# Buffers at multiples of 64 bytes, later triangular solves, two low parts on VectorE and modulation slabs first, in a hybrid transformer layer

## The chip, the cores and the metric

The kernel runs on one NeuronCore of a Trainium2 chip. The metric is the device time of one execution in microseconds (us), lower is better. The kernel before takes 1467.25 us, the median of 3 runs (1467.24 to 1467.57).

## The reference, cut to what matters

One layer mixes a latent stream of 1024 tokens and a context of 256 tokens, width 1024, all in fp32. `w_in` projects the normalised input to three head groups; `w_out` joins them; a squared-ReLU MLP of width 4096 follows.

```python
mod = silu(c) @ w_mod + b_mod            # six rows of 1024: sh1, sc1, g1, sh2, sc2, g2
h = rms(x, norm1) * (1 + sc1) + sh1      # the same for the context with c_ctx
P = project(h, w_in)                     # f (256) | aq (512) | ak, av (128 each) | dq, dk, dv (256 each) | dz (256) | gates (16)
# Gated DeltaNet on dq, dk, dv: centred conv + SiLU, chunks, one scan per direction
tmat = triangular_solve(eye + lmat, eye) # lmat from k k^T and the decays
o_dn = scan over the chunks, in both directions, from the context's final state
o_att = softmax(q k^T / 8) v             # 8 query heads, 2 kv heads, over latent and context keys
x = x + g1 * (concat(dft2(f), o_att, gated_norm(o_dn)) @ w_out)
x = x + g2 * (relu(h2 @ w_ff1) ** 2 @ w_ff2)
```

## The kernel before, in words

**Number format.** A product in near-fp32 is made of three matmuls in the fast format fp32r: each operand is split into a high part (the value rounded to fp32r) and a low part (what is left), and `mm3` (L238) issues high by high, high by low and low by high into one PSUM bank. In the trace they are L239, L240 and L241. A matmul streams its moving operand (the right one of `mm`/`mm3`, up to 512 columns) past 128 columns of weights (the left one).

**Memory.** Four regions of SBUF hold everything. `fbase` (FW words of 4 bytes) and `rbase` (RW words, fp32r) lie one behind the other, `z1a` (later `z1b`, `z1c`, `z1d`; Z1W words) follows them, `z2a` (later `z2b`, `z2c`; Z2W words) is laid against the upper end. Each is an `Arena`, which hands out buffers at multiples of 8 words, that is 32 bytes (`words`, L115). In the built program `fbase` begins at byte 16512 of a partition, so `rbase` begins at 16512 + 4 x 16200 = 81312, `z1a` at 81312 + 4 x 18704 = 156128, and `z2a` at 190432. Only `fbase` begins at a multiple of 64; the three others lie 32 bytes past one, and the operands of all fp32r matmuls are in these three. Their buffers there have sizes of whole multiples of 64 bytes, so each moving operand and each block of weights begins 32 bytes past a multiple of 64, either at 32 or at 96 of 128.

**Stages**, in the order of time (us of the profiled span):

- 0 to 60: the modulation. `w_mod` comes as slabs of 128 rows by 1024 columns (512 KB each), eight for each of the six output rows (`mod_steps`, L314); a slab feeds four matmuls of 256 columns (L321 is its DMA). The first two row blocks of x are loaded (`load_x`, L362, DMA L365), normalised (`norm_in`) and transposed (L244, into `xTb`) between the slabs of the first output row (q = 0), whose result is sh1; q = 1 gives sc1. From both comes `hT`, the modulated input, transposed, high and low.
- 60 to 200: the projections of `w_in`. `wgroup` (L434) loads a group of 256 or 272 columns in two halves, ScalarE makes the high part (`act`, L223), and the engine `eng` the low part (a subtraction of 128 x 1024, L446). `proj_N` (L474) and `proj_T` (L463) are the matmul loops; each calls `tick` (L453), which advances the generators in `tasks`.
- From the second half of the query columns on, `tasks` has `systems` (L764) and `system1` (L772). `systems` first yields GRAM = 4 times, then makes the Gram blocks of the keys (`grams`: matmuls L734 of 32 x 32, scaled on VectorE in L737, sent to DRAM), then solves the triangular systems of direction 0 on VectorE; `system1` waits for the Gram blocks and solves direction 1 on GpSimd. Each solve (`solve`, L745) has 30 steps of a product (L758) and a sum (L759), first for the context (32 partitions), then for the latent tokens (128 partitions). Beside them VectorE, GpSimd and ScalarE normalise and rotate the query rows (`qk_rows`, L502: L508 to L520).
- 200 to 340: `w_dv` and `w_dq`, the value and query columns of the DeltaNet group, with low parts on GpSimd (`wgroup(..., G)`), their convolutions (L594 to L603 on VectorE, matmuls L627), then the columns dz and f (`wfz`, `dz_f`), whose group f is prepared once both solves of the context and the 4 first steps of `dz_f` are issued.
- 340 to 705: attention (scores of 256 columns, values of 512 columns by 65 weights, row maxima of 512 columns, all fp32r in `rbase`) with the DeltaNet scan (fp32 matmuls of 32 to 64) in between.
- 705 to 850: `w_out` (moving operand in `z1c`, 256 columns) and the Fourier group. 850 to 1155: the first MLP product (weights in `z1c`, moving operand in `rbase` or `z2b`, 512 columns). 1155 to 1450: the second (both in `rbase`, 512 columns).

**What sets the order.** A scheduler orders the instructions of each engine by program order, priorities and its own estimate of when operands are ready; matmuls under `pinned` and DMAs under `ypin` keep the order of the program. Each engine then works off its queue in order, and an instruction that waits holds all behind it.

Of the kernel before, what the change touches and what calls it, by code (L numbers as in the profile page):

```python
# [17 lines left out]
P = 128  # L18
D = 1024
# [3 lines left out]
KT = D // P  # L23
# [7 lines left out]
NCC = CTX // CK  # L31
NCA = NCL + NCC
EPS = 1e-6
FW, RW, Z1W, Z2W = 16200, 18704, 8576, 9728

COL_F, COL_AQ, COL_AK, COL_DQ, COL_DK, COL_DV, COL_DZ, COL_G = 0, 256, 768, 1024, 1280, 1536, 1792, 2048

# [2 lines left out]
NGP = ((0, 3), (122, 140))  # L40
OFF = 800
OFN = 1000
GRAM = 4
PIN = lambda i: i
HOPS = (0, 5, 7, 9, 10, 11, *range(13, 33, 2))
FIRST = 2
# [63 lines left out]
class Arena:  # L110
# [2 lines left out]
        self.typed = base.dtype  # L113

    def words(self, n, top=False):  # L115
        n = (n + 7) // 8 * 8
        order = range(len(self.free_) - 1, -1, -1) if top else range(len(self.free_))
        for q in order:
            a, b = self.free_[q]
            if b - a >= n:  # L120
                if top:
                    at = b - n
                    self.free_[q] = (a, at)
                else:
                    at = a
                    self.free_[q] = (a + n, b)
                self.used[at] = n
                self.peak = max(self.peak, sum(self.used.values()))
                return at
        raise RuntimeError(f"arena full: {n} words, free {self.free_}, used {sorted(self.used.items())}")  # L130
# [64 lines left out]
def body(tc, t, out):  # L195
# [3 lines left out]
    with ctx:  # L199
# [9 lines left out]
        zp2, Z2 = zone("right", Z2W, F32, "z2a")  # L209
# [4 lines left out]
        V, G, T, Y, SC = nc.vector, nc.gpsimd, nc.tensor, nc.sync, nc.scalar  # L214

        def buf(*shape, top=False, a=None, at=None):
            return Buf(a or Fa, (P,) + shape, top, at)
# [14 lines left out]
        def yd(i):  # L232
            return tc.keep_in_program_order(i) if ypin else i

        def mm(o, l, r, start, stop):
            pe(T.matmul(o, l, r, start=start, stop=stop))  # L236
# [37 lines left out]
        cs = csb()  # L274
# [10 lines left out]
        at = 16  # L285
# [24 lines left out]
        def mod_pass(*a):  # L310
            for _ in mod_steps(*a):
                pass

        def mod_steps(q, slabs, bank, queue=Y, many=1):  # L314
            w = t["w_mod"]
            for k in range(KT):
                sl = slabs.next()
                sl = sl if isinstance(sl, tuple) else (sl,)
                n = D // len(sl)
                for z, part in enumerate(sl):  # L320
                    yd(queue.dma_start(part, w[0, k * P : (k + 1) * P, q * D + z * n : q * D + (z + 1) * n]))  # L321
                for g in range(4):
                    mm(bank[32 * g : 32 * g + 32, 0:256], cs[:, k, :], sl[g * 256 // n][:, g * 256 % n : g * 256 % n + 256], k == 0, k == KT - 1)
                if k % many == many - 1:
                    yield

# [12 lines left out]

        rowtmp = buf(256)  # L340
        slab0 = [buf(D, a=Z2) for _ in range(8)]
        slabs = Ring([b() for b in slab0])

# [60 lines left out]
        ypin = True  # L406
        xs0 = load_x(t["x"][0], 0, xb[0:2])
        norm_in(xs0)
        slab1 = [buf(D, a=Z2)]
        xTb = [buf(256) for _ in range(KT)]  # L410
        trb = Ring([bk[0], bk[1]])
        slabs = Ring([b() for b in slab0 + slab1])
        for k, _ in enumerate(mod_steps(0, slabs, bk[2])):
            b = trb.next()
            for q, xt in enumerate(xs0):
# [74 lines left out]
        ypin = False  # L490
# [60 lines left out]
        for p, xs in enumerate((xs1, xs2, xs3, xs4)):  # L551
            norm_in(xs)
            g, c0 = ((0, 256), (1, 0), (1, 256), (2, 0))[p]
# [108 lines left out]
        b = gb.next()  # L662
# [9 lines left out]
        b = gb.next()  # L672
# [8 lines left out]
        b = gb.next()  # L681
# [5 lines left out]
        for d in range(2):  # L687
# [3 lines left out]
            for c in range(0, NCA, 16):  # L691
                n = min(16, NCA - c)
# [103 lines left out]
            proj_N(w_q, 256, range(NT), q_sink(half))  # L796
        for b in [x for r in rt.items for x in r] + rst.items + stg.items + [gqk]:
            b.free()
        w_dv = wgroup([(COL_DV, 256)], G)
        conv_proj(w_dv, 0, (0, 1, 2))  # L800
        dst = conv_silu(0, 4, (0, 1, 2), "v", 0)
        conv_proj(w_dv, 1, (0, 1, 2))
# [5 lines left out]
        wlo.items.append(rbuf(4, 256, a=Z1))  # L808
        wb += [whi.items[-1], wlo.items[-1]]
        whi.at = wlo.at = 2  # L810
        w_dq = wgroup([(COL_DQ, 256)], G)
        conv_proj(w_dq, 1, (0, 1))
        compact(dst, 1, VC, 0.5)
        G.tensor_tensor(VC, VC, NK[:, 0].unsqueeze(2).to_broadcast([P, NCA, HD]), op=ALU.mult)
# [987 lines left out]
```

## Time and profile before

| | |
|---|---|
| median of 3 runs | 1467.25 us |
| the profiled execution | 1465.56 us |
| its span | 1463.8 us |
| mean granted TensorE clock | 0.979 |
| TensorE busy (matmuls) | 1385.7 us, 95% of the span |
| VectorE, ScalarE, GpSimd busy | 1003.7, 704.8, 673.4 us |
| bytes moved by DMA | 197.67 MB, 135 GB/s over the span |

The span is what the profiler saw from the first to the last instruction; the execution is 1.8 us longer than it. Busy time of a matmul row runs from its issue to its modelled end, and rows overlap: 0.39 us is one matmul's length, but what it takes of the engine is the distance between two starts. The columns of a table by stretch are busy us of PE, PEld, DVE, ACT and POOL (with instruction counts), the granted TensorE clock (1.00 is 2.4 GHz, 0.50 is 1.2 GHz), the DMA engines' busy share and GB/s.

### The profile page before, as it was taken

Reading aid. Unit: us, or ns where it says so; the run is one execution under the profiler, and the core shown is the slowest. Engines: PE = TensorE matmul, PEld = TensorE weight load, DVE = VectorE, ACT = ScalarE, POOL = GpSimd, SP = SyncE. Lnnn points to the kernel's source line nnn. Section 1 sums busy time; section 2 is a strip of 40 time slices with the busy share of each in tenths; the row PEclk is TensorE's granted clock in tenths of the full one; section 3 lists DMA queues with packets and bytes.
Section 4 is the critical chain, followed back from the end, with each engine's and each line's share of the span. In section 5 each row is a group of like instructions: output and inputs, shape, how many; then the busy total and the mean of one; then the engine's idle time right before and its main releaser. Section 6 shows DMA issues by size and latency. Waiting matters only on the chain.

```text
span 1463.8 us, 28936 instructions
## 1 busy us (share of the span) xinstructions
PE 1385.7 (95%) x11462; PEld 1119.9 (77%) x11462; DVE 1003.7 (69%) x1691; ACT 704.8 (48%) x1239; POOL 673.4 (46%) x743
## 2 busy tenths in 40 slices
PE   5899968899999999989899899999999999999998
PEld 1677967676777777768799777888888888888886
DVE  0774589965888777786723788655556677676994
ACT  1742412233777777767512664555455443443331
POOL 2653778783446456465533724444433100010782
PEclk8899989899999999999999999999999999999999
DMA  8873151233000010042222215544446897766641
GB/s 315 315 271 123 34 115 36 66 85 90 9 10 24 9 32 10 9 149 64 84 93 93 104 60 163 178 130 149 150 159 205 302 394 263 245 225 219 201 159 58
DMA packets 137304, 197.67 MB, mean 135 GB/s; under 512 B 45021, under 2 KB 80463, under 8 KB 136911
## 3 DMA queue, kind: packets, MB, share of 16 engines
q1 hardware_dynamic: 136464, 195.12, 40.8%
q8 instruction: 90, 1.47, 0.4%
q10 hardware_dynamic: 703, 0.69, 0.2%
q14 instruction: 47, 0.39, 0.1%
HBM read 149.84 MB, written 45.94 MB: 134 GB/s over the span
## 4 chain that ended last, share of the span: by engine, by line
PE 48%; DVE 2%; POOL 2%; DMA 1%; issue 1%; ACT 0%; DVEq 0%; SPq 0%; POOLq 0%; ACTq 0%
PE bk L240 8%; PE bk L239 8%; PE bk L241 8%; PE ba L239 7%; PE ba L240 7%; PE ba L241 7%; PE bk L236 2%; DVE z1b L1333 0%; PE ba L236 0%; POOL rbase L1468 0%; DMA fbase<-x 0%; PE bk L244 0%; DVE rbase L996 0%; POOL z2c L1734 0%; POOL z2c L1732 0%
## 5 line engine op out<-in xcount | busy, mean ns | idle before, releaser
L223 ACT ACTIVATE rbase<-fbase 128x512 fp32r<-128x512 f32 (+3 forms) x255 | 171.7, 686 | 88.0 <-PE bk L240 55.6
L223 ACT ACTIVATE fbase<-bk 128x512 f32<-128x512 f32 (+3 forms) x224 | 125.0, 561 | 142.7 <-PE bk L236 94.0
L236 PE MATMUL bk<-rbase 128*128 128x256 f32 (+2 forms) x984 | 173.1, 311 | 4.6 <-ACT fbase L223 2.5
L236 PEld LDWEIGHTS bk<-rbase 128*128 128x128 f32 (+1 forms) x984 | 132.2, 175 | 34.2 <-ACT fbase L223 3.3
L236 PE MATMUL ba<-rbase 128*65 128x512 f32 (+4 forms) x576 | 138.4, 342 | 6.2 <-DVE rbase L996 4.8
L223 ACT ACTIVATE z1c<-fbase 128x512 fp32r<-128x512 f32 (+1 forms) x120 | 76.7, 653 | 134.9 <-DMA fbase<-w_ff 51.0
L223 ACT ACTIVATE fbase<-fbase 128x512 f32<-128x512 f32 (+4 forms) x148 | 96.0, 659 | 91.9 <-POOL fbase L1624 27.5
L1501 POOL TENSOR_TENSOR fbase<-fbase 128x512 f32<-128x512 f32 x64 | 87.4, 1367 | 114.5 <-DVE z1c L1468 89.5
L1706 POOL TENSOR_TENSOR z2c<-z2c,fbase 128x512 f32<-128x512 f32 x16 | 31.1, 1968 | 204.6 <-ACT z2c L223 128.5
L972 DVE TENSOR_REDUCE fbase<-ba 128x1 f32<-128x512 f32 (+1 forms) x192 | 106.4, 593 | 19.5 <-PE ba L236 18.1
L223 ACT ACTIVATE rbase<-z1d 128x1024 fp32r<-128x1024 f32 x61 | 63.0, 1055 | 101.3 <-PE bk L240 86.6
L1468 DVE TENSOR_TENSOR z1c<-fbase,z1c 128x512 fp32r<-128x512 f32 x112 | 91.2, 818 | 24.0 <-ACT z1c L223 20.8
L1468 DVE TENSOR_TENSOR rbase<-z1d,rbase 128x1024 fp32r<-128x1024 f32 x61 | 85.1, 1411 | 27.7 <-ACT rbase L223 27.2
L996 POOL TENSOR_TENSOR rbase<-fbase,rbase 128x512 fp32r<-128x512 f32 x56 | 72.1, 1288 | 67.0 <-ACT rbase L223 62.9
L239 PE MATMUL bk<-rbase 128*128 128x512 f32 x256 | 99.6, 389 | 0.0
L240 PE MATMUL bk<-rbase 128*128 128x512 f32 x256 | 99.6, 389 | 0.0
L241 PE MATMUL bk<-rbase 128*128 128x512 f32 x256 | 99.6, 389 | 0.0
L996 DVE TENSOR_TENSOR rbase<-fbase,rbase 128x512 fp32r<-128x512 f32 x104 | 81.5, 784 | 25.5 <-ACT rbase L223 25.1
L1468 DVE TENSOR_TENSOR rbase<-fbase,rbase 128x1024 fp32r<-128x1024 f32 (+1 forms) x65 | 81.3, 1269 | 21.2 <-ACT rbase L223 21.0
L236 PEld LDWEIGHTS ba<-rbase 128*65 128x65 f32 (+1 forms) x576 | 76.1, 155 | 24.1 <-DVE rbase L996 5.9
L240 PE MATMUL ba<-rbase 128*128 128x512 f32 x192 | 74.7, 389 | 0.0
L241 PE MATMUL ba<-rbase 128*128 128x512 f32 x192 | 74.7, 389 | 0.0
(350 smaller groups left out, 3823.5 us busy)
## 6 DMA issues: line engine op xcount, KB each, us to landing
fbase<-w_ff SPq DMA_DIRECT2D x70, 512.0 KB
u<-fbase SPq DMA_DIRECT2D x112, 256.0 KB
z2a<-w_mod SPq DMA_DIRECT2D x36, 512.0 KB
z1d<-w_ff SPq DMA_DIRECT2D x34, 512.0 KB
z1d<-u SPq DMA_DIRECT2D x33, 512.0 KB
fbase<-u SPq DMA_DIRECT2D x23, 512.0 KB
fbase<-w_in SPq DMA_DIRECT2D x16, 512.0 KB
fbase<-x SPq DMA_DIRECT2D x14, 512.0 KB
```

The source lines that it names most:

```text
L223: return SC.activation(o, i, f, **k)
L236: pe(T.matmul(o, l, r, start=start, stop=stop))
L239: pe(T.matmul(o, lh, rh, start=start, stop=False))
L240: pe(T.matmul(o, lh, rl, start=False, stop=False))
L241: pe(T.matmul(o, ll, rh, start=False, stop=stop))
L972: V.tensor_reduce(st4[:, z : z + 1], b, AX.X, ALU.max)
L996: (G if k2 in GP and not any(a <= n < b for a, b in NGP) else V).tensor_tensor(hl[:, :, 1], p, f32(hl[:, :, 0]), op=ALU.subtract)
L1468: eng.tensor_tensor(lo, i, f32(hi), op=ALU.subtract)
L1501: G.tensor_tensor(w[nm], w[a], w[b], op=op)
L1706: G.tensor_tensor(c, c, G2[cs_.start // 512], op=ALU.mult)
```

## The change

Four edits.

1. **Addresses.** FW is 16192 and Z2W is 9736, and an arena hands out buffers of 64 words or more at multiples of 16 words (64 bytes). `rbase` now begins at 81280, `z1a` at 156096, `z2a` at 190400, all multiples of 64, so every operand of an fp32r matmul moves 32 bytes down, from 32 or 96 of 128 to 0 or 64 of 128. Which pairs of moving operand and weights have the same place of 128, and which differ by 64, stays as it was.
2. **Later solves.** GRAM is 15.
3. **Low parts.** `w_dv` and `w_dq` use the default engine of `wgroup`, VectorE: four subtractions (L446) leave GpSimd.
4. **Slabs first.** The ninth slab buffer is there from the start, and the eight slabs of q = 0 are loaded ahead of the first row blocks of x.

```diff
-FW, RW, Z1W, Z2W = 16200, 18704, 8576, 9728
+FW, RW, Z1W, Z2W = 16192, 18704, 8576, 9736
...
-GRAM = 4
+GRAM = 15
...
     def words(self, n, top=False):
+        unit = 16 if n >= 64 else 8
         n = (n + 7) // 8 * 8
         order = range(len(self.free_) - 1, -1, -1) if top else range(len(self.free_))
         for q in order:
             a, b = self.free_[q]
-            if b - a >= n:
-                if top:
-                    at = b - n
-                    self.free_[q] = (a, at)
-                else:
-                    at = a
-                    self.free_[q] = (a + n, b)
+            at = (b - n) // unit * unit if top else -(-a // unit) * unit
+            if at >= a and at + n <= b:
+                self.free_[q : q + 1] = [x for x in ((a, at), (at + n, b)) if x[0] < x[1]]
...
+        early = {}
+
+        def slab_load(q, k, slabs, queue=Y):
+            sl = slabs.next()
+            yd(queue.dma_start(sl, t["w_mod"][0, k * P : (k + 1) * P, q * D : (q + 1) * D]))
+            return sl
+
         def mod_steps(q, slabs, bank, queue=Y, many=1):
-            w = t["w_mod"]
             for k in range(KT):
...
+                sl = slab_load(q, k, slabs, queue) if (q, k) not in early else early.pop((q, k))
                 for g in range(4):
-                    mm(bank[32 * g : 32 * g + 32, 0:256], cs[:, k, :], sl[g * 256 // n][:, g * 256 % n : g * 256 % n + 256], k == 0, k == KT - 1)
+                    mm(bank[32 * g : 32 * g + 32, 0:256], cs[:, k, :], sl[:, g * 256 : g * 256 + 256], k == 0, k == KT - 1)
...
         slab0 = [buf(D, a=Z2) for _ in range(8)]
-        slabs = Ring([b() for b in slab0])
+        slab1 = [buf(D, a=Z2)]
+        slabs = Ring([b() for b in slab0 + slab1])
+        ypin = True
+        for k in range(KT):
+            early[0, k] = slab_load(0, k, slabs)
+        ypin = False
...
-        slab1 = [buf(D, a=Z2)]
         xTb = [buf(256) for _ in range(KT)]
         trb = Ring([bk[0], bk[1]])
-        slabs = Ring([b() for b in slab0 + slab1])
...
-        w_dv = wgroup([(COL_DV, 256)], G)
+        w_dv = wgroup([(COL_DV, 256)])
...
-        w_dq = wgroup([(COL_DQ, 256)], G)
+        w_dq = wgroup([(COL_DQ, 256)])
```

**SyncE's DMA queue at the start of the program.** Before, the rows of x come ahead of the slabs of `w_mod`:

```order
L365 DMA fbase<-x 128x1024 x2
L321 DMA z2a<-w_mod 128x1024 x12
L321 DMA fbase<-w_mod 128x1024
L321 DMA z2a<-w_mod 128x1024 x4
L442 DMA fbase<-w_in 128x4x256
```

Now (line numbers are the changed kernel's: L315 is a slab, L369 a row block of x, L444 a half of a weight group):

```order
L315 DMA z2a<-w_mod 128x1024 x8
L369 DMA fbase<-x 128x1024 x2
L315 DMA z2a<-w_mod 128x1024 x7
L315 DMA fbase<-w_mod 128x1024
L315 DMA z2a<-w_mod 128x1024
```

Eight slabs now go ahead of the two row blocks. The four halves of the first weight group follow the sixteenth slab as before.

**The low parts of `w_dq`.** Before, they stand on GpSimd, in the twenty-first step of its solve for the context (a step is a pair L758 and L759; 32x210 is the size of the twenty-first product):

```order
L758 TENSOR_TENSOR fbase<-z2a 32x220
L759 TENSOR_TENSOR z2a<-z2a,fbase 32x20x11
L758 TENSOR_TENSOR fbase<-z2a 32x210
L446 TENSOR_TENSOR z1a<-fbase,z1a 128x1024
L759 TENSOR_TENSOR z2a<-z2a,fbase 32x21x10
L446 TENSOR_TENSOR z1a<-fbase,z1a 128x1024
L758 TENSOR_TENSOR fbase<-z2a 32x198
```

Now they stand on VectorE (L448), in the twenty-fourth step of its solve for the context (L760 and L761):

```order
L760 TENSOR_TENSOR fbase<-z2a 32x168
L923 TENSOR_SCALAR rbase<-fbase 128x10
L448 TENSOR_TENSOR z1a<-fbase,z1a 128x1024
L761 TENSOR_TENSOR z2a<-z2a,fbase 32x24x7
L913 TENSOR_SCALAR rbase<-fbase 128x136
L448 TENSOR_TENSOR z1a<-fbase,z1a 128x1024
L760 TENSOR_TENSOR fbase<-z2a 32x150
```

The two low parts of `w_dv` move likewise, to the fifth step of VectorE's solve.

**The low parts of the group f on VectorE.** Before, they stand behind the last step of the solve for the latent tokens (128 partitions):

```order
L758 TENSOR_TENSOR fbase<-fbase 128x84
L759 TENSOR_TENSOR fbase<-fbase 128x28x3
L758 TENSOR_TENSOR fbase<-fbase 128x58
L759 TENSOR_TENSOR fbase<-fbase 128x29x2
L758 TENSOR_TENSOR fbase<-fbase 128x30
L759 TENSOR_TENSOR fbase<-fbase 128x30
L446 TENSOR_TENSOR z1a<-fbase,z1a 128x1024 x2
```

Now eleven steps of that solve come behind the first of them:

```order
L760 TENSOR_TENSOR fbase<-fbase 128x228
L761 TENSOR_TENSOR fbase<-fbase 128x19x12
L448 TENSOR_TENSOR z1a<-fbase,z1a 128x1024
L760 TENSOR_TENSOR fbase<-fbase 128x220
L761 TENSOR_TENSOR fbase<-fbase 128x20x11
L760 TENSOR_TENSOR fbase<-fbase 128x210
L448 TENSOR_TENSOR z1a<-fbase,z1a 128x1024
L761 TENSOR_TENSOR fbase<-fbase 128x21x10
```

On TensorE the first Gram block moves behind 96 matmuls of 256 columns of the second half of the query columns that it stood ahead of.

## Rows read from the trace of the kernel before

**Rows 1.** The page: the chain of work that ended last, share of the span by engine.

```profile
PE 48%; DVE 2%; POOL 2%; DMA 1%; issue 1%; ACT 0%; DVEq 0%; SPq 0%; POOLq 0%; ACTq 0%
```

**Rows 2.** Busy time by stretch: attention, first MLP product, second MLP product.

```profile
350.00:700.00 350.00, 341.29 (x4725) 264.56 (x4715) 269.59 (x624) 249.48 (x501) 184.80 (x218) 1.00 0.12 36
...
850.00:1155.00 305.00, 304.41 (x1309) 244.04 (x1308) 196.71 (x288) 156.90 (x268) 124.66 (x88) 1.00 0.48 156
1155.00:1450.00 295.00, 295.00 (x1304) 244.33 (x1303) 212.02 (x173) 115.41 (x120) 68.02 (x34) 1.00 0.68 233
```

**Rows 3.** TensorE's timeline, second product: start us, us, instruction; first and fifteenth.

```profile
1199.72 0.39 PE L241 MATMUL bk<-rbase 128*128 128x512 f32 x1
...
1202.89 0.39 PE L240 MATMUL ba<-rbase 128*128 128x512 f32 x1
```

**Rows 4.** TensorE's timeline, first product: nine steps from z2b, then seven from rbase.

```profile
999.72 0.39 PE L239 MATMUL bk<-z2b,z1c 128*128 128x512 f32 x1
...
1001.76 0.39 PE L239 MATMUL bk<-rbase,z1c 128*128 128x512 f32 x1
...
1003.39 0.39 PE L240 MATMUL bk<-rbase,z1c 128*128 128x512 f32 x1
```

**Rows 5.** TensorE's timeline, fp32 matmuls of 256 columns, two recorded passes each.

```profile
663.92 0.59 PE L236 MATMUL bk<-fbase,z1b 128*128 128x256 f32 x2
...
664.78 0.59 PE L236 MATMUL bk<-fbase,z1b 128*128 128x256 f32 x2
```

**Rows 6.** TensorE's timeline, fp32r matmuls of 256 columns in w_out; six steps apart.

```profile
789.94 0.28 PE L241 MATMUL bk<-z1c,rbase 128*128 128x256 f32 x1
...
790.62 0.28 PE L241 MATMUL bk<-z1c,rbase 128*128 128x256 f32 x1
```

**Rows 7.** TensorE's groups by shape, 345 to 705: count, busy us, mean ns.

```profile
L236 PE MATMUL bk<-rbase 65*128 65x256 f32 x306 | 80.5, 284 | 0.0
...
L236 PE MATMUL ba<-rbase 128*65 128x512 f32 x152 | 61.8, 424 | 1.4 <-DVE rbase L996 1.4
...
L236 PE MATMUL ba<-rbase 128*128 128x512 f32 x124 | 45.0, 404 | 1.1 <-DVE fbase L972 0.9
```

**Rows 8.** TensorE's groups by shape, 705 to 850: one of six alike.

```profile
L241 PE MATMUL ba<-z1c,z2b 128*128 128x256 f32 x92 | 26.0, 283 | 0.0
```

**Rows 9.** TensorE's groups by shape, 60 to 200: one of three alike.

```profile
L239 PE MATMUL ba<-z1a,rbase 128*128 128x256 f32 x69 | 20.1, 294 | 0.0
```

**Rows 10.** TensorE's waits, 180 to 330: us in total, times, longest.

```profile
PE ba L239 <- ACT z1a L223: 7.1, 1, 7.1
PE bk L241 <- POOL z1a L446: 6.5, 1, 6.5
PE bk L627 <- DVE fbase L601: 5.7, 1, 5.7
PE bk L241 <- DVE z1a L446: 3.2, 1, 3.2
PE ba L241 <- POOL z1a L446: 2.8, 1, 2.8
```

**Rows 11.** Busy time by stretch: ten us in the midst of the solves.

```profile
220.00:230.00 10.00, 10.00 (x50) 8.36 (x50) 9.70 (x23) 2.69 (x6) 7.19 (x11) 0.92 0.21 72
```

**Rows 12.** VectorE's timeline: a late step of the solve, then the low parts of f.

```profile
306.19 0.63 DVE L758 TENSOR_TENSOR fbase<-fbase 128x30 f32<-128x30 f32 x1
...
306.97 3.21 DVE L446 TENSOR_TENSOR z1a<-fbase,z1a 128x1024 fp32r<-128x1024 f32 x2
```

**Rows 13.** All low parts by engine: ns min/median/max, first and last start us.

```profile
L446 DVE TENSOR_TENSOR z1a<-fbase,z1a x12: 1216/1252/1664, 39.4 to 308.6; 128x1024 fp32r<-128x1024 f32 x10, 128x1088 fp32r<-128x1088 f32 x2
...
L446 POOL TENSOR_TENSOR z1a<-fbase,z1a x4: 2339/2510/3660, 177.6 to 257.4; 128x1024 fp32r<-128x1024 f32 x4
```

**Rows 14.** Busy time by stretch: the front, 15 to 20.

```profile
15.00:20.00 5.00, 3.05 (x20) 1.18 (x19) 1.64 (x3) 0.66 (x2) 1.45 (x3) 1.00 0.59 197
```

**Rows 15.** TensorE's timeline: the last slab that the input waits for.

```profile
36.52 0.64 PE L236 MATMUL bk<-z2a,fbase 128*32 128x256 f32 x8 [0.66 <-DMA z2a<-w_mod]
```

More of the change, by code (lines that the diff above doesn't have):

```diff
@@ L312, in mod_pass @@
                 pass
+        early = {}
[3 more added lines that the diff above has]
+            return sl
         def mod_steps(q, slabs, bank, queue=Y, many=1):
-            w = t["w_mod"]
             for k in range(KT):
[L317 to L321, printed above, removed]
+                sl = slab_load(q, k, slabs, queue) if (q, k) not in early else early.pop((q, k))
                 for g in range(4):
-                    mm(bank[32 * g : 32 * g + 32, 0:256], cs[:, k, :], sl[g * 256 // n][:, g * 256 % n : g * 256 % n + 256], k == 0, k == KT - 1)
+                    mm(bank[32 * g : 32 * g + 32, 0:256], cs[:, k, :], sl[:, g * 256 : g * 256 + 256], k == 0, k == KT - 1)
                 if k % many == many - 1:
```

## The prediction

> **What bounds the kernel now.** I read the chain of work first, then busy time by stretch, then TensorE's own timeline. In the chain [rows 1] TensorE stands for 48% of the span and no other engine for more than 2%. The stretches say where that holds: from 850 to 1450 TensorE is busy 304.4 of 305 and 295 of 295 us, in attention 341.3 of 350, while VectorE, the next busiest, has 212 of 295 and 270 of 350 [rows 2]. The granted clock there is 1.00, 2.4 GHz. So over two thirds of the time each nanosecond between two matmul starts counts, and nothing else does. Between 200 and 310 it is different: VectorE is 97% busy [rows 11] and TensorE has its long waits there [rows 10]. The front, 0 to 60, waits for DMA [rows 14, 15].
>
> The reader should now look at the distance between starts rather than at the 0.39 us of a row. In the second product fifteen starts lie 3.17 us apart in 14 steps: 226.4 ns, 543.5 cycles at 2.4 GHz for 512 columns [rows 3]. That is 30 to 32 cycles too many, one for each 64 bytes of the 2048 that a partition streams. In the first product the step is (1001.76 - 999.72) / 9 = 226.7 ns with the moving operand in `z2b`, but (1003.39 - 1001.76) / 7 = 232.9 ns with it in `rbase` [rows 4]. Same engine, same columns, same clock, same weights' buffer: only the place differs. In the one case moving operand and weights have the same place of 128 bytes, in the other they differ by 64. So addresses do matter to a matmul's rate here. For 256 columns the step is 0.68 / 6 = 113.3 ns, 272 cycles, again 16 too many [rows 6]. Against these stand fp32 matmuls, whose passes take twice the cycles for a column: four passes in 664.78 - 663.92 = 0.86 us, 215 ns for 512 cycles' work [rows 5]. There the stream asks for half the bytes in a cycle, and the extra is gone. What is left of fixed cost is 215.0 - 213.3 = 1.7 ns.
>
> **Addresses.** All fp32r operands lie 32 bytes past a multiple of 64, and none of the trace lies on one; the price of an aligned matmul is therefore not in the trace and must be bounded. Lower price: that of rows 5, 215 ns for 512 columns, and 106.7 + 1.7 = 108.4 for 256; below it nothing is left to save at this clock. Upper price: today's 226.4 and 113.3, the stream of 4-byte columns simply being so slow. Dearer than today is bounded by the 232.9 ns of the conflicting pairs, but the change keeps each pair's difference, which speaks against that. I take the lower price: the excess is a whole cycle for each 64 bytes, what a read would cost whose 64 bytes always straddle a boundary, and the change takes away exactly the straddling. The saving is then 11.4 ns for 512 columns and 4.9 for 256, and it counts where TensorE is the bound:
> - second product: 1304 matmuls [rows 2] x 11.4 = 14.9 us;
> - first product: 1309 x 11.4 = 14.9; the other 6 ns of those from `rbase` I leave in place, since the difference of 64 stays;
> - attention: scores 2 x 306 and 363 other ones of 256 columns x 4.9 = 4.8, and 152 + 150 + 124 of 512 x 11.4 = 4.9 [rows 7] (one row for each kind);
> - `w_out`: six groups of 92 [rows 8] and four of 36, 696 x 4.9 = 3.4;
> - projections of 60 to 200: three groups of 69, 68 and 68 and three of 48 with 256 columns, 349 x 4.9 = 1.7, and about 1.3 for those of 272 and 512 (an estimate from the same price) [rows 9].
> Together 46 us. Elsewhere TensorE waits anyway. Other engines become no bound by it: at 5% less time VectorE's 212 of 295 is 76%. No tile of theirs costs me anything for its address; I found no difference in their durations between places at 0 and at 32 of 64.
>
> The Trainium skill ("TensorE: Matmul & The Clock Gate", section "Wait — 56ns, not 53.3ns?") gives the start-to-start distance of warm matmuls as N / 2.4 GHz plus about 2.5 ns, 215.7 ns for 512 columns, whatever the place of the operands. The 226.4 and 232.9 of rows 3 and 4 disagree, the 215 of rows 5 agrees; by 215.7 as the aligned price the sum of this part would be 43 instead of 46.
>
> **Low parts and later solves (180 to 320).** The change takes four subtractions off GpSimd, 2.51 us each [rows 13], and puts them on VectorE at 1.25 each, 5.0 us more in a queue without a gap. It also pushes back the Gram blocks behind 96 matmuls of 256 columns (96 x 0.113 = 10.9 us) and with them all solves. What it removes by name: the wait of 7.1 for ScalarE's high part of `w_dv`, whose inputs stood behind query rows that VectorE worked off between solve steps, and the waits of 6.5 and 2.8 for GpSimd's low parts [rows 10], 16.4 us. That can't all be kept, because VectorE's queue is the bound: what counts is how much of its work stands ahead of the low parts of f, the last thing that TensorE waits for (3.2). Eleven steps of the solve for the latent tokens, 22 instructions of about 0.63 [rows 12], 13.9 us, go behind them; the four new subtractions, 5.0, come ahead. 5.0 - 13.9 = -8.9; as subtractions beside a busy GpSimd take up to 1.66 [rows 13], 4 x 0.4 of it is lost again: -7.3. I take -8. Ends: -16.4, all named waits gone, and 0, where the convolutions (5.7 for L601) wait as long as now and hold what follows. That the 22 steps run later costs nothing as long as VectorE has room after 310; what would be late next are the solves' results, a rival below. Behind a waiting low part on VectorE stand solve steps, for which TensorE does not wait.
>
> **Slabs first.** The first slabs no longer wait behind the rows, and the hole of 15 to 20, where the DMA engines have 0.59 [rows 14], can close: 0.41 x 5 = 2.0 us, which the last slab [rows 15], on the path to the first projection, comes sooner. The row blocks land eight slabs later, about 8 x 1.3 = 10 us by the distance of slabs, still well before the sixteenth. I take -2; ends -4 (the waits for slabs around it too) and +2 (the rows' transposes becoming late).
>
> **Sum.** 1465.56 - 46 - 8 - 2 = 1409.6 us against the profiled execution; that one lies 1.7 below the median of the runs, so 1411 in their terms.
>
> **The rivals.** *The stream is so slow whatever the address* (A2). For it: with 4 bytes for each column no row shows the full rate, and rows 5 differ from rows 3 in format too. Against it: rows 4, where a place changes the rate. Then only 10 us go: 1465.6 - 10 + 1.7 = 1457. *Only half of it* (A3): the boundary is 128 bytes, so operands now at 64 of 128 keep their cycle, or the pairs that differ by 64 keep more than today: 46 / 2 off, 1434. *Solves late* (B), the other side: addresses give nothing, and the solves, begun 10.9 us later, end on GpSimd later too, so that attention, whose buffers are those which the solves give back, starts later by as much. For it: 60 steps on each engine follow the last Gram block without a break. Against it: GpSimd is freed of 4 x 2.51 = 10.0 us in the same stretch. It decides from the point where the last solve step ends later than TensorE's last matmul of the f columns. Price up to 10.9: 1465.6 + 10.9 - 2 + 1.7 = 1476. *The change not doing what it says* can be ruled out in part: the three regions' first bytes are multiples of 64 by the sizes given, and the order shows the other edits.
>
> A rule of the Trainium skill that would favour A2 is on the same page, section "Step-by-step: what each phase is for": TensorE reads moving operand and weights through two independent ports, so that loading weights takes nothing from a running matmul. The 226.7 against 232.9 of rows 4 disagrees with it in this kernel.
>
> **How the numbers follow.** My forecast has 0.63, A3 0.08, A2 0.22, B 0.07. The forecast's own range is 1394 (the first product's 6 ns and all named waits gone too: 1411 - 9 - 8) to 1428 (215.7 as the price, nothing from the solves, +2 in front, and some 4 us of TensorE time that other engines give back as waits). It holds 0.58 of the whole; with A3 and the half of A2 that lies below 1457.5 the range 1394 to 1458 holds about 0.78. Runs of this kernel can tell 0.2%, 2.9 us, from no change. Faster than 1464.3: the forecast, A3, and most of A2, 0.88; within 2.9 us: the rest of A2, 0.05; slower: B, 0.07.
>
> **What would show it.** Right: steps of 215 ns in the second product, 215 to 222 in the first, and 108 in `w_out`; 600 us of MLP shorter by 30; TensorE's waits in 180 to 330 down to about 19 us, with VectorE as the one waited for, and no wait for a slab above 1 us after the first. Wrong: steps of 226 again, which leaves 10 us; steps above 227, which would be a new conflict and a slower kernel; or a gap on TensorE at the start of attention.

## The result, and the profile after

The changed kernel takes 1456.26 us (5 runs, 1455.26 to 1460.07) against 1467.25 (5 runs, 1462.12 to 1467.73): ratio 0.9941, 95% interval 0.9923 to 0.9958. By that ratio it is 8.7 us or 0.6% faster (the two medians alone lie 11.0 us apart). That is far from the 1411 of the forecast and within 1 us of the rival A2, 1457.

The page of the changed kernel: span, busy time by engine, the chain that ended last.

```profile
span 1454.5 us, 28942 instructions
...
PE 1384.1 (95%) x11462; PEld 1117.6 (77%) x11462; DVE 1005.7 (69%) x1695; ACT 703.6 (48%) x1239; POOL 668.5 (46%) x739
...
PE 47%; DVE 2%; POOL 2%; DMA 1%; issue 1%; ACT 1%; SPq 0%; DVEq 0%; POOLq 0%; ACTq 0%
```

TensorE's busy time is 1.6 us less, where the forecast took 46 us off it. Its stretches answer to [rows 2]:

```profile
850.00:1155.00 305.00, 304.40 (x1310) 244.42 (x1309) 193.46 (x280) 155.06 (x262) 124.22 (x88) 1.00 0.50 167
1155.00:1450.00 295.00, 292.18 (x1290) 241.72 (x1288) 214.77 (x178) 112.16 (x117) 75.17 (x40) 1.00 0.67 226
```

305 us still hold 1310 matmuls of the first product, 1309 before; in the second stretch the kernel now ends before 1450. TensorE's timeline says the same (start us, us, instruction): in the second product fifteen starts, as in [rows 3].

```profile
1199.72 0.39 PE L237 MATMUL bk<-rbase 128*128 128x512 f32 x1
...
1202.89 0.39 PE L236 MATMUL ba<-rbase 128*128 128x512 f32 x1
```

And in the first product, as in [rows 4], twelve steps from `z2b`, then four from `rbase`:

```profile
989.74 0.39 PE L236 MATMUL bk<-z2b,z1c 128*128 128x512 f32 x1
...
992.46 0.40 PE L236 MATMUL bk<-rbase,z1c 128*128 128x512 f32 x1
...
993.40 0.39 PE L237 MATMUL bk<-rbase,z1c 128*128 128x512 f32 x1
```

(1202.89 - 1199.72) / 14 = 226.4 ns, (992.46 - 989.74) / 12 = 226.7, (993.40 - 992.46) / 4 = 235: nothing of what the addresses were to give. The waits of TensorE from 180 to 330, against [rows 10]:

```profile
PE bk L238 <- DVE z1a L448: 9.9, 3, 6.0
PE ba L238 <- DVE z1a L448: 3.5, 1, 3.5
PE bk L629 <- DVE fbase L603: 2.3, 1, 2.3
PE bk L736 <- DVE z2a L739: 2.2, 1, 2.2
```

25.3 us of waits for ScalarE, GpSimd and VectorE (26.9 with 1.6 in the Gram blocks) have become 17.9, all for VectorE. The low parts that were GpSimd's [rows 13] are VectorE's (ns min/median/max, first and last start):

```profile
L448 DVE TENSOR_TENSOR z1a<-fbase,z1a x16: 1204/1222/1702, 39.9 to 299.1; 128x1024 fp32r<-128x1024 f32 x14, 128x1088 fp32r<-128x1088 f32 x2
```

To see where the time was won I compared the start of TensorE's matmul number k in both traces, both having 11462 of them (worked out from the two traces; us; the last two columns are two of the experiments below, against the same trace of before):

```
    k   before   after-before   later+lows (e7)   same 512 (e10)   what stands there
  400     77.0        -0.1           -0.7             -1.1         projections
 1900    202.6        -0.5           -1.7             -1.0         the Gram blocks are done
 2000    233.9        -7.9           -9.7            -10.9         w_dv
 2300    277.9       -11.7          -12.7            -13.7         w_dq
 2700    323.2       -10.7          -15.1            -12.8         the columns f
 3100    350.9       -10.4           -4.5            -12.5         attention begins
 8600    806.0        -9.3           -6.1            -11.4         end of w_out
10200   1170.3        -9.3           -6.1            -17.3         second product begins
11400   1442.3        -9.3           -6.1            -17.3         its end
```

All of the gain lies between 200 and 280; the front gives 0.1 us, the two products give nothing. Nearly all of it is waits: from number 1900 to 2300 TensorE waits 22.1 us before (the 7.1, 6.5, 5.7 and 2.8 of [rows 10]) and 11.8 now (6.0, 3.5 and 2.3), 10.3 of the 11.2 us won there.

### The profile page after: what moved, and what is told of

Read it like the earlier page. It is cut to its first block, busy times and chain, and to the rows that moved or that the text cites. A ratio compares the mean times of both kernels' runs of the same rounds, so it can differ in the third digit from the quotient of the medians.

```text
span 1454.5 us, 28942 instructions
## 1 busy us (share of the span) xinstructions
PE 1384.1 (95%) x11462; PEld 1117.6 (77%) x11462; DVE 1005.7 (69%) x1695; ACT 703.6 (48%) x1239; POOL 668.5 (46%) x739
## 4 chain that ended last, share of the span: by engine, by line
PE 47%; DVE 2%; POOL 2%; DMA 1%; issue 1%; ACT 1%; SPq 0%; DVEq 0%; POOLq 0%; ACTq 0%
PE bk L237 8%; PE bk L238 8%; PE bk L236 8%; PE ba L236 7%; PE ba L237 7%; PE ba L238 7%; PE bk L233 1%; DVE z1b L1335 0%; PE ba L233 0%; DMA fbase<-w_out 0%; POOL rbase L1470 0%; DMA fbase<-la 0%; DMA la<-fbase 0%; DVE rbase L998 0%; POOL z2c L1734 0%
## 5 line engine op out<-in xcount | busy, mean ns | idle before, releaser
L998 DVE TENSOR_TENSOR rbase<-fbase,rbase 128x512 fp32r<-128x512 f32 x104 | 80.5, 774 | 25.7 <-ACT rbase L220 25.3
```

The costliest lines, as they stand in the source:

```text
L998: (G if k2 in GP and not any(a <= n < b for a, b in NGP) else V).tensor_tensor(hl[:, :, 1], p, f32(hl[:, :, 0]), op=ALU.subtract)
```

## The experiments

Three kernels leave out the layer and run groups of matmuls alone; all others compute the whole layer. The number of a group's step is the mean distance of starts in it, from the trace.

**e1: the step for many places.** Per group: `for _ in range(24): matmul(bank, wt[:, w : w + 128], mv[:, m : m + n])`, no other engine at work.

> This kernel computes nothing of the layer: it leaves all of it out and only runs groups of 24 equal matmuls one behind the other, one group for each pair of places of the moving operand and the weights (in bytes of 128), with 512, 256 and 128 columns, with fewer columns of weights, in bf16, in fp32 and with every second column, while the other engines stand still. Read is the distance between two starts within a group. Theory A (the stream of 4-byte columns in fp32r loses one cycle in 17 whatever its address, as the changed kernel's 226.7 ns at places 0 and 0 says): all fp32r groups with moving and weights at one place take 226.7 ns, bf16 groups 215 to 216 at any place, the group with every second column not less than 226. Theory B (only the difference of the two places counts, and some difference not tried in the two kernels avoids the loss): a difference of 16, 32 or 48 gives 214 to 216 ns while 0 gives 226.7 and 64 gives 233. Theory C (the loss comes from the other engines and DMAs that share the memory): 214 to 216 ns at all places, since they are idle. Theory D (it is the load of the next weights that takes cycles from the stream): the loss falls with the columns of weights, to 222 ns with 64 and about 219 with 32.

```
512 columns, fp32r: places of moving / weights in bytes of 128, ns
 0/0 226.7   0/8 230.8   0/16 233.4   0/32 233.4   0/64 233.2   0/96 233.9
 32/32 228.4 (settles at 227)   32/96 233.4   64/64 228.7 (settles at 227)   64/0 229.0   96/96 227.7
 8/8 231.7   16/16 231.0 (neither settles at 227)   16/0 231.6
 64 partitions instead of 128: 0/0 232.3 (settles at 227)   0/64 233.4
 weights of 96, 64, 32 columns at 0/0: 231.2, 230.0, 232.1
bf16, 512 columns: 0/0 215.8   0/64 215.8
fp32, 256 columns, one pass: 215.8     fp32r, every second column of 1024: 452
fp32r, 256 columns: 0/0 119.8   0/64 113.4   96/32 117.9   64/64 120.2
fp32r, 128 columns: 0/0 109.3   0/64 111.7
```

Two groups of the timeline, one behind the other, show how the reader gets such a number: places 0/0 (24 starts in 18.01 - 12.57 = 5.44 us) and, later, 8/8 (112.29 - 106.72 = 5.57). Where the table says that a group settles, the number is the mean of its second half.

```profile
12.57 5.60 PE L38 MATMUL b<-mv,wt 128*128 128x512 f32 x24
18.01 5.60 PE L39 MATMUL b<-mv,wt 128*128 128x512 f32 x24
...
106.72 5.73 PE L55 MATMUL b<-mv,wt 128*128 128x512 f32 x24
112.29 5.71 PE L56 MATMUL b<-mv,wt 128*128 128x512 f32 x24
```

Theory C falls: with all else idle the step is the kernel's. D falls: fewer columns of weights save nothing. B falls: no difference of 8 to 96 bytes gives 215. Of A the main point stands: at no place does an fp32r group settle below 226.6 ns. 0/0 and 32/32 settle alike, as the kernel's second product does before and after the change, so reads that straddle a boundary of 64 bytes aren't the cause. But A's "at one place 226.7" is too simple: with both operands 8 or 16 bytes past a multiple of 32 the step stays at 231, so the place itself does matter there. Half the partitions change nothing. And a hint on the cause: running over twice the bytes, with every second column, takes twice the time.

**e5: bytes or format.** The same, with the moving operand `mv[:, 0:1]` broadcast to 512 columns, 64 or 16 columns repeated, every second or fourth column, in bf16 and fp32, and every third or fourth in fp32r.

> Again groups of 24 equal matmuls and nothing of the layer. The first such kernel gave 226.7 ns for 512 columns in fp32r at equal places, 215.8 in bf16 and in the passes of fp32, and about 452 with every second fp32r column. Theory A1 (the limit is how many bytes of memory the stream runs over in a time, 64 bytes in 17 cycles): fp32r with one column repeated 512 times, or with 64 or 16 columns repeated, takes 214 to 216 ns; bf16 with every second column, which runs over 2048 bytes, takes 226 to 234 instead of 215.8, bf16 with every fourth about 452; fp32 with every second column 215 to 234 for a pass, with every fourth about 452 for two or one. Theory A2 (the format fp32r itself takes 17 cycles for 16 columns): repeated columns stay at 226.7, bf16 with every second column stays at 215.8. 384 columns: 170 ns (17 cycles for 64 bytes) at equal places, and 170 to 175 at places 64 apart.

```
512 columns, ns                              run over by the stream, bytes of a partition
 fp32r 226.7                                  2048
 fp32r, one column repeated 218.6                4
 fp32r, 64 columns repeated 227.6               256, eight times
 fp32r, 16 columns repeated 242.0                64, 32 times
 fp32r, every third 471.5 (last half 464), every fourth 461.4     6144, 8192
 bf16 215.8, every second 225.8, every fourth 451.6     1024, 2048, 4096
 fp32 (256 columns), a pass: 215.8, every second 227.1, every fourth 451     1024, 2048, 4096
 fp32r, 384 columns: places 0/0 174.4, 64 apart 176.7     1536
```

In the timeline 24 starts with every third fp32r column take 72.09 - 60.78 = 11.31 us, 471 ns each, with every fourth 83.19 - 72.09 = 11.10, 462 ns; for the pass in fp32 with every second column there are 48 starts in 94.09 - 83.19 = 10.90 us, 227.1 ns:

```profile
60.78 11.51 PE L46 MATMUL b<-mv,wt 128*128 128x512 f32 x24
72.09 11.27 PE L47 MATMUL b<-mv,wt 128*128 128x512 f32 x24
83.19 11.06 PE L48 MATMUL b<-mv,wt 128*128 128x256 f32 x48
94.09 21.81 PE L49 MATMUL b<-mv,wt 128*128 128x256 f32 x48
```

A2 falls: bf16 becomes as slow as fp32r when its columns lie 4 bytes apart, and fp32r drops to 218.6 when it need not advance. So the excess goes with how far apart the columns lie, not with the format. A1 fits only in part. Over 2048 bytes of each partition the groups take 226 to 227 ns, over 4096 twice that. But fp32r over 6144 and 8192 bytes takes 464 and 461, where A1's 17 cycles for 64 bytes would need 680 and 907, and 16 columns repeated take longer than all 512. What limits the stream is therefore not shown; what is measured is its rate as `mm3` uses it: 2048 bytes in 226.7 ns, 9.0 bytes a ns, against the 9.6 that 4 bytes at 2.4 GHz would need.

**e2: the addresses alone.** The kernel before with `FW, RW, Z1W, Z2W = 16192, 18704, 8576, 9736` and the new `words`.

> The kernel before with only the first edit, all buffers of 64 words or more at multiples of 64 bytes. Theory A and B (the place of both operands moves alike, so nothing changes): ratio 1.000, steps of 226.7 and 233 ns as before, the end within 1 us of before's. The prediction's theory (straddling reads) would need 1467 - 46 = 1421 us; the changed kernel's steps already speak against it. If the regions' new bytes changed anything else (VectorE, DMA), it would show here as more than 2 us.

Ratio 1.0016 (0.9999 to 1.0032), 1468.5 us in 10 runs; in its trace the step is 226.7 ns in the second product and 233.3 in the first from `rbase`. The first edit by itself is worth nothing, or 2 us the wrong way.

**e3 and e4: one edit on the solves' side each.**

```diff
-GRAM = 4
+GRAM = 15
```

> The kernel before with only the second edit, GRAM 15 instead of 4. Theory S (the query rows of VectorE come ahead of the solves, so ScalarE's high part of w_dv is no longer late; VectorE's queue stays the bound): the wait of 7.1 us for ScalarE goes, the start of attention comes 4 to 8 us sooner. Rival L (the gain is that of the low parts; later solves alone only push the waits for GpSimd's low parts back, since those stand between solve steps): less than 3 us, with longer waits for GpSimd's low parts than 6.5 and 2.8 us.

Ratio 0.9951 (0.9932 to 0.9970). TensorE's waits from 180 to 330 in its profile:

```profile
PE bk L627 <- DVE fbase L601: 7.4, 1, 7.4
PE ba L241 <- POOL z1a L446: 4.2, 1, 4.2
PE bk L734 <- DVE z2a L737: 2.9, 1, 2.9
PE bk L241 <- POOL z1a L446: 2.9, 1, 2.9
PE bk L241 <- DVE z1a L446: 2.0, 1, 2.0
```

The 7.1 for ScalarE [rows 10] is gone, attention begins 5.5 us sooner: Theory S.

```diff
-        w_dv = wgroup([(COL_DV, 256)], G)
+        w_dv = wgroup([(COL_DV, 256)])
...
-        w_dq = wgroup([(COL_DQ, 256)], G)
+        w_dq = wgroup([(COL_DQ, 256)])
```

> The kernel before with only the third edit, the low parts of w_dv and w_dq on VectorE. Theory S: the 7.1 us wait stays, the waits for GpSimd (6.5 and 2.8 us) become waits for VectorE of about the same size, 0 to 3 us sooner. Rival L: 5 to 10 us sooner with these alone.

Ratio 0.9962 (0.9948 to 0.9977), attention 3.5 us sooner in the profile. Theory S is off here: the 7.1 us became 1.1 too, without later solves, the 3.5 us lie above its 0 to 3, and the 5.6 us that the ratio gives (3.4 to 7.6) lie inside the 5 to 10 of rival L.

```profile
PE bk L241 <- DVE z1a L446: 10.2, 2, 6.0
PE bk L627 <- DVE fbase L601: 7.4, 2, 4.2
PE ba L241 <- DVE z1a L446: 3.1, 1, 3.1
...
PE ba L239 <- ACT z1a L223: 1.1, 1, 1.1
```

**e7: both of them**, at the old addresses and with the old front.

> The kernel before with the second and third edit, GRAM 15 and the low parts on VectorE, at the old addresses and with the old front. Alone they gave ratios of 0.9951 and 0.9962. Theory S (both work on one thing, VectorE's queue ahead of the low parts of f, so they don't add up): 0.993 to 0.995, TensorE at its 3100th matmul 8 to 11 us sooner, as in the changed kernel. If they add up: 0.9913, 13 us sooner.

Ratio 0.9978 (0.9963 to 0.9994), 3.2 us (0.9 to 5.4): less gained than with either alone, though the intervals overlap, and not the 0.993 to 0.995 of theory S. The table of matmul starts shows why: 15.1 us are won by number 2700, and by 3100 only 4.5 are left, 10.6 are given back. The waits there (300 to 340) come to 3.7 us; the rest goes with the clock, in the busy time by stretch:

```profile
PE bk L614 <- ACT fbase L223: 2.6, 1, 2.6
PE bk L244 <- DMA tsc<-fbase: 1.1, 1, 1.1
```

```profile
313.50 0.39 DVE L759 TENSOR_TENSOR fbase<-fbase 128x30 f32<-128x30 f32 x1
...
317.59 1.01 PE L614 MATMUL bk<-fbase 64*32 64x2 f32 x32 [2.64 <-ACT fbase L223]
```

```profile
310.00:320.00 10.00, 7.36 (x62) 5.62 (x61) 8.00 (x14) 4.31 (x8) 9.11 (x19) 0.88 0.48 83
320.00:330.00 10.00, 8.92 (x114) 6.33 (x113) 3.25 (x8) 3.60 (x8) 0.36 (x2) 0.50 0.76 143
330.00:340.00 10.00, 10.00 (x121) 6.45 (x121) 4.69 (x10) 1.34 (x3) 5.57 (x2) 0.77 0.66 183
```

After the wait, which ends at 317.6, the granted clock is 0.50 (1.2 GHz) through the twenties, though TensorE is busy for 8.9 of those 10 us. The wait leads back to VectorE: its solve ends at 313.9 (in the kernel before at 307.1), the last instruction of a convolution (L601) stands behind it and ends at 316.4, then comes ScalarE's square, then TensorE. In the changed kernel VectorE ends that instruction (L603 there) at 317.0; TensorE comes 4.4 us later, has no wait and a clock of 1.00 from 310 to 340. The 10.6 us are near rival B's price of 10.9, but not by B's mechanism: GpSimd's solve ends at 320.3 here, 320.4 in the changed kernel and 330.0 before, so it is earlier and not later, and most of the 10.6 us is paid in clock.

**e6: slabs first alone.** The kernel before with the fourth edit (the diff's `early`, `slab_load` and ring of nine).

> The kernel before with only the fourth edit, the eight slabs of the first output row ahead of the rows of x. The changed kernel's trace had TensorE at the same matmul 0.1 us earlier at 77 us, so: Theory F (what the slabs gain, the rows' path gives back before the first projections are through): ratio 0.999 to 1.001, the 400th matmul within 0.5 us of before's. The prediction's term: 2 us sooner from 40 us on to the end.

Ratio 1.0001 (0.9984 to 1.0018), the 400th matmul 0.4 us later than before's. Theory F. In the changed kernel the hole of [rows 14] is still there, SyncE's queue waits for TensorE before it issues two of the slabs (waits of SyncE, 0 to 60; in the kernel before it waited 7.9 us for TensorE before one), and TensorE waits for slabs behind the rows:

```profile
15.00:20.00 5.00, 2.42 (x25) 0.76 (x23) 0.23 (x1) 0.00 (x0) 0.00 (x0) 1.00 0.64 200
```

```profile
SPq L315 <- PE bk L233: 5.4, 2, 4.8
```

```profile
20.86 0.64 PE L233 MATMUL bk<-z2a,fbase 128*32 128x256 f32 x8 [2.83 <-DMA z2a<-w_mod]
22.01 0.44 PE L241 MATMUL bk<-fbase 128*128 128x128 f32 x2 [0.51 <-ACT fbase L220]
26.11 1.08 PE L233 MATMUL bk<-z2a,fbase 128*32 128x256 f32 x8 [3.67 <-DMA z2a<-w_mod]
...
37.78 0.64 PE L233 MATMUL bk<-z2a,fbase 128*32 128x256 f32 x8
```

Its first slab is used at 6.64 instead of 11.84, its last at 37.78 instead of 36.52 [rows 15].

**e8: equal places of 128.** The changed kernel with other sizes of the regions, all four summing to the same:

```diff
-FW, RW, Z1W, Z2W = 16192, 18704, 8576, 9736
+FW, RW, Z1W, Z2W = 16160, 18720, 8576, 9752
```

> The changed kernel with the four regions at 16160, 18720, 8576 and 9752 words, so that rbase, z1a and z2a all begin at a multiple of 128 bytes; the order of the instructions is the same on all engines. Moving operand and weights of the first MLP product then lie at one place of 128 instead of 64 apart. Theory P (equal places let the stream fall into steps of 226.7 ns, others stay at 233): the 1317 matmuls of 512 columns between rbase and z1c save 6.6 ns each, 8.7 us, of which the 1309 of the stretch of the first product hold nearly all of the 850 with rbase, 5.6 us, and the projections the rest; the 768 of 256 columns in w_out, 64 apart now, lose 2 to 6 ns each, 1.5 to 4.6 us. Sum 3 to 6 us faster than the changed kernel, ratio to before 0.990 to 0.992. Rival (the difference of the steps comes from something else in these stages): no change against the changed kernel, 0.994.

Ratio 0.9943 (0.9921 to 0.9966), as the changed kernel; steps from `rbase` still 232 ns. Theory P falls. Working out the places of 512 for each pair of operands showed what P had overlooked: the pairs at 226.7 were equal of 512 as well, those of e8 at 128 or 384.

**e9: how far apart.**

> Groups of 48 equal fp32r matmuls and nothing of the layer: 512 columns, then 256, with the weights 0, 64, 128, 192, 256, 320, 384, 448, 512, 640, 768, 1024, 1536 and again 0 bytes behind the place of the moving operand (taken of 512). In the whole kernel the pairs of rbase and z1c took 233 ns at 64 apart of 512, and 232 at 128 apart (equal of 128); the pairs that take 226.7 are equal of 512. Theory Q (the steps settle at 226.7 ns only where both operands have the same place of 256 or of 512): 226.7 at 0, 512, 1024, 1536 (and 256, 768 if it is 256), 231 to 234 at the others. Theory P (equal of 128 is enough): 226.7 at 128, 256, 384, 640 too. With 256 columns, by the first run: 120 at 0, 113 to 118 at others.

```
fp32r, weights so many bytes behind the moving operand's place; ns, mean of the last 24 steps
512 columns:  0 226.7  64 233.3  128 232.7  192 228.9  256 226.7  320 233.3  384 232.7  448 228.9
              512 226.7  640 232.1  768 226.7  1024 226.7  1536 226.7
256 columns:  0 120.0  64 117.8  128 118.7  192 117.8  256 119.8  320 117.8  448 117.8  512 120.0
```

Theory Q, with a period of 256 bytes, though 192 and 448 apart (228.9) are better than its 231 to 234. With 256 columns, 64 apart, the step is 117.8 here and was 113.4 in e1 for the same two places; why isn't known. In the timeline, 48 starts in 73.13 - 62.23 = 10.90 us for 256 apart, 84.33 - 73.13 = 11.20 for 320:

```profile
62.23 11.06 PE L42 MATMUL b<-mv,wt 128*128 128x512 f32 x48
73.13 11.36 PE L43 MATMUL b<-mv,wt 128*128 128x512 f32 x48
84.33 11.32 PE L44 MATMUL b<-mv,wt 128*128 128x512 f32 x48
```

**e10: equal places of 512, in the whole kernel.**

```diff
-FW, RW, Z1W, Z2W = 16192, 18704, 8576, 9736
+FW, RW, Z1W, Z2W = 16192, 18688, 8576, 9752
```

> The changed kernel with regions of 16192, 18688, 8576 and 9752 words, so that rbase, z1a and z2a begin at one place of 512 bytes; TensorE's order is the same. Theory Q: the 1170 matmuls of 512 columns between rbase and z1a or z1c that are then equal of 512 save 6.6 ns each, 804 of them in the first product's stretch, 5.3 us, the others partly hidden; the 561 of 256 columns between z1c and rbase lose about 2.5 ns, 1.4 us. Sum 4 to 6 us faster than the changed kernel, ratio to before about 0.991; steps of 227 in the first product from rbase too. If the steps stay at 232 to 233: no change, 0.994.

1449.6 us, ratio 0.9889 (0.9871 to 0.9908), faster than both kernels. The first product from `rbase`, sixteen steps: (983.40 - 979.77) / 16 = 226.9 ns.

```profile
979.77 0.39 PE L238 MATMUL ba<-rbase,z1c 128*128 128x512 f32 x1
...
983.40 0.39 PE L236 MATMUL ba<-z2b,z1c 128*128 128x512 f32 x1
```

Between numbers 8600 and 10200 of the table it wins 5.9 us that the changed kernel doesn't, for the 5.3 expected.

**e11: the changed kernel without the first edit.**

> The changed kernel without the first edit: GRAM 15, low parts on VectorE and slabs first at the old addresses. Edits two and three alone gave 0.9978, because a wait of 2.6 us for ScalarE and one of 1.1 us for DMA before attention let TensorE's clock fall to half for some 16 us; the changed kernel has full clock there. Theory O (the front or the order that comes with it keeps TensorE fed there): 0.993 to 0.995 without the first edit too. Rival (the first edit, by which buffer lies where, changes the order there): 0.997 to 0.999, with the clock at half before attention.

Ratio 0.9960 (0.9937 to 0.9983), 8 runs from 1452.12 to 1463.74. Its interval takes in both answers. In the profiled execution the clock before attention does fall (mean 0.90 from 300 to 350, after a wait of 2.4 us for a DMA), but the fastest run lies below all of the changed kernel's. Inconclusive.

**e12: later still.** The changed kernel with `GRAM = 26`.

> The changed kernel with GRAM 26. Theory S (VectorE's queue ahead of the low parts of f is the bound; what goes behind them is free): TensorE's waits between 180 and 330 fall from 18 us to 12 to 16, ratio 0.990 to 0.994. Rival B (the solves are late next: attention waits for their buffers and results): a wait of 3 us or more, or half clock, between 310 and 345, ratio 0.996 or above.

Ratio 1.0014 (1.0002 to 1.0027): the gain is gone. By number 2600 TensorE is 17.6 us ahead of before, more than in any other kernel, by 3000 it is 1.2 behind. Waits and busy time from 300 to 350:

```profile
PE bk L616 <- ACT fbase L220: 7.5, 1, 7.5
PE bk L241 <- issue: 3.9, 1, 3.9
```

```profile
300.00:350.00 50.00, 38.62 (x483) 27.21 (x485) 29.11 (x54) 11.18 (x23) 25.25 (x37) 0.76 0.47 111
```

```profile
316.87 0.34 DVE L761 TENSOR_TENSOR fbase<-fbase 128x30 f32<-128x30 f32 x1
...
317.46 1.29 DVE L603 SCALAR_TENSOR_TENSOR z2a<-fbase 128x1024 f32<-128x1024 f32 x1
```

Theory S's 0.990 to 0.994 is missed; the signs of rival B (a long wait, half the clock, 0.996 or above) came, but again by way of VectorE. Its solve ends at 317.2, the end of the convolution (L603) at 318.8, ScalarE's square follows, and then the wait of 7.5 us ends. GpSimd's solve ends at 321.7, 8.3 us sooner than in the kernel before. It can have a part in the second wait, 3.9 us, for which the profile names no releaser: the rows that TensorE transposes there are loaded by a DMA that SyncE issues at 325.6, right behind the stores of that solve. So in this kernel later solves help as long as VectorE is done with its own when TensorE needs what stands behind it.

## Why the prediction was wrong, point by point

**Addresses: -46 us, measured 0 (e2: +2, interval 0 to +5).** The step that failed is the choice between the bounds: "I take the lower price: the excess is a whole cycle for each 64 bytes, what a read would cost whose 64 bytes always straddle a boundary". The upper price was the true one, 226.4 and 113.3 ns as before. With all other engines idle the excess is still there, at every place tried (e1, no group of 512 fp32r columns settles below 226.6), and it goes with the distance of the columns rather than with the format (e5: bf16 at 4 bytes a column 225.8). Why the stream runs at 9.0 bytes a ns stays open. The row that could have told it was [rows 5], and it was read the right way at first ("the stream asks for half the bytes in a cycle, and the extra is gone"); the conclusion drawn from it was that 215 is the aligned price, where it was only the price of half the bytes. A second row stood right beside [rows 6], in `w_out` of the kernel before: six steps with the weights in `z2b`, at the same place as the moving operand.

```profile
790.73 0.28 PE L239 MATMUL bk<-z1c,z2b 128*128 128x256 f32 x1
...
791.45 0.28 PE L239 MATMUL bk<-z1c,rbase 128*128 128x256 f32 x1
```

(791.45 - 790.73) / 6 = 120.0 ns, 288 cycles: 32 too many for 1024 bytes, two for each 64 bytes and not one. The prediction took the 113.3 of the pairs 64 apart for all matmuls of 256 columns. [rows 4] were the second mistake: they show that a place matters, but the place of one operand relative to the other, and the prediction itself said that the change keeps each pair's difference. An observation that the change doesn't touch can't carry a term of its sum.

The Trainium skill ("TensorE: Matmul & The Clock Gate", section "Wait — 56ns, not 53.3ns?") agrees with the bf16 groups, 215.8 against its 215.7, but not with fp32r, 226.7. The Trainium skill's two independent ports (same page, section "Step-by-step: what each phase is for"), by which loading weights takes nothing from a running matmul, fit e1's groups with fewer columns of weights, which are no faster. They don't fit e9, where the place of the weights alone moves the step from 226.7 to 233.3.

**Low parts and later solves: -8 us; measured -3.2 by themselves (e7, -5.4 to -0.9), in the changed kernel's profile -9.3 with the front's 0.1.** The mechanism held in the changed kernel: the waits named went or became VectorE's, 17.9 us against the "about 19" forecast, and VectorE's last low part starts at 299.1 instead of 308.6 [rows 13], 9.5 us sooner for the 7.3 to 8.9 of the working. The two parts don't add up (0.9951 and 0.9962 alone, 0.9978 together at the old addresses). That they cost the clock before attention in e7, and not in the changed kernel's profile, is a measured difference whose cause e11 doesn't settle. So the three terms measured by themselves (e2 +2, e7 -3, e6 0) don't add up to the -8.7 of the whole, and that the whole comes out near the 8 of this term is partly luck.

**Slabs first: -2 us, measured 0 (e6: -2 to +3).** The hole didn't close: some slabs' issue still waited for TensorE, 5.4 us in all (the ring's buffers come free with its matmuls), and the transposes of the rows, now later, stand between the last slabs, from 22 to 39. Which of the two counts more was not tried. "Still well before the sixteenth" was right for the landing of the rows, and not enough: norm, transposes and slabs share TensorE and the ring.

**Rivals.** A2 was the case, at 0.22, and its 1457 was right, with the luck just told in its -10. B, at 0.07, isn't what this change does. Solves that come too late are real (e7 a little, e12 in full, about 10 us), but it is VectorE's solve that holds what TensorE needs; GpSimd's end, which B went by, came sooner than before in both. A3 is out: no half of the term exists.

## What to carry to other kernels

Before an address is moved, ask whether the rows compare absolute places or two operands' places relative to each other, and whether the change alters what they compare. A stream's rate is tested in a few us: halve or double the bytes it runs over and keep the columns. Work that is pushed back on a full engine is free only until its own consumer comes due; look for the point (here a first wait with GRAM 15 in e7, the whole gain gone with 26 in e12), and read the granted clock beside the waits, as waits of 3.7 us cost 10.6.

## What the runs showed that I had not expected

- A matmul of 512 fp32r columns, with 128 columns of weights, has the step 226.7 ns where moving operand and weights have the same place of 256 bytes and begin at the multiples of 32 that were tried, 228.9 to 233.9 else (231 with both 8 or 16 bytes past one), and needs four to ten matmuls to settle after a change. With 256 columns equal places are the slower ones, 120 against 117.8 (e9) or 113.4 (e1) 64 apart. Sixteen words taken from one region and given to another were worth 0.5% of the whole kernel.
- A repeated column isn't free: one column streamed 512 times takes 218.6 ns, not 215.8, and 16 columns repeated 242. And a wider distance isn't always dearer: in fp32r every second column takes 452, every fourth 461.
- The same kernel before gave 1459 to 1470 us over the 19 to 22 runs that stood beside the experiments; effects under 3 us can be told here by the matmul starts of two traces better than by the times.
